# A mixture-of-experts stage on one core: 32-row blocks for the ranks with fewest tokens, 64 + 32 rows for middle ranks, and another order of experts

## The chip, the cores and the metric

The kernel runs on one core of one Trainium2 chip. The metric is device time in microseconds (us). Before the change the median of three runs is 1831.31 us (1824.54 to 1831.61). The profile is of one further execution, which took 1831.17 us; its first to last instruction span 1829.4 us.

## The reference

One decoder layer over 512 tokens of width 1024: two token mixers and a projection, a layer norm, then 32 experts of which each token takes 4, and a layer norm. The change concerns the experts alone.

```python
def moe_ffn(x2d, router_w, router_b, w1, b1, w2, b2):
    logits = (x2d @ router_w + router_b).astype(jnp.float32)      # 512 x 32
    top_logit, top_idx = lax.top_k(logits, TOP_K)                 # TOP_K = 4
    gate = jax.nn.softmax(top_logit, axis=-1)
    ...
    def expert_block(acc, blk):
        tok, w, e = blk
        h = x_pad[tok] @ w1[e] + b1[e]                            # 1024 -> 2048
        g, lin = jnp.split(h, 2, axis=-1)
        g = jnp.minimum(g, SWIGLU_LIMIT)
        lin = jnp.clip(lin, -SWIGLU_LIMIT, SWIGLU_LIMIT)
        act = g * jax.nn.sigmoid(SWIGLU_ALPHA * g) * (lin + 1.0)
        y = act @ w2[e] + b2[e]                                   # 1024 -> 1024
        return acc.at[tok].add((w[:, None] * y).astype(acc.dtype)), None
```

With the inputs of `setup_inputs()` the experts, expert 0 last and the others by falling count, have 179, 176, 152, 115, 106, 94, 89, 89, 85, 73, 73, 67, 61, 60, 57, 56, 54, 53, 48, 41, 40, 35, 34, 30, 28, 25, 20, 19, 18, 16, 15 and 40 tokens.

## The kernel before

A front part (until about 604 us) computes the mixers, the layer norm and the router. `Router.order` ranks experts 1 to 31 by their number of tokens; rank 31 (`FIRST`) is expert 0, which is always worked on first because its number is known ahead. `moe` then goes through the 32 ranks in the order that the string `TURNS` writes out (h heavy, m middle, l light). All weights are float32.

Each expert's weights come in 12 **units** of 1 MB, 8 of w1 and 4 of w2, fetched by SyncE's queue (SP) in the order in which they are used, into a ring of eight buffers (`Units.fetch`, L251; the tiles are called `raw` and, for two of the eight, `hl`). A **turn** is one pass of the main loop (L460): the first w1 half of this expert (4 units), two w2 units of the expert before, the second w1 half (4 units), the other two w2 units of the expert before. So a turn holds 8 units of its own expert and 4 of the expert of the turn ahead of it.

The tokens of an expert stand in **blocks** (`blocks`). A *full* block has 128 rows. Its operands are split into a high and a low float32r part: ScalarE makes the high part (L271), VectorE the low one (L274), and TensorE does three products of them (`PASS`), 12 matmuls of 128x512 for a unit (L392). A *half* block has 64 rows: 64 columns of TensorE hold the rows, the two halves of the outputs go to columns 0 to 63 and 64 to 127 at the same time, plain float32, no split (L380). A buffer is free again when a half block's matmuls, or a full block's split, have read it.

Before the change rank 0 has two full blocks, ranks 1 to 3 a full and a half block, ranks 4 to 12 and `FIRST` one full block, ranks 13 to 30 one half block. In the order of the turns: F l m l h l m l l h l m l m l h l m l l m l h l m l m l l m l l.

For each block `gather` builds a one-hot of the tokens (L320, VectorE), turns it into row numbers by four small matmuls (L325), and fetches the rows by an indirect DMA of GpSimd (L338) into the one tile `xg`; `turn` transposes them on TensorE (L360 half, L369 full). `swiglu` runs on VectorE and ScalarE (L425 to L430). `send` copies the product (L449) and adds it to the rows of `ysum` in DRAM by an indirect DMA (L450), all 128 partitions, 512 KB for a full block and 256 KB for a half one. `bias2` (after the first turn) adds the gated b2 rows. `early` (after the second) counts the tokens and writes a table (`overflow_table`) of experts with more tokens than their blocks hold; `overflow`, a loop behind the main one, runs once for each entry of the table.

Of the kernel before, what the change touches and what calls it, by code (L numbers as in the profile page):

```python
# [27 lines left out]
def moe_consts(nc, cp):  # L28
    c = {}
    ident = cp.tile([P, P], F32, name="ident")  # L30
    nc.gpsimd.memset(ident, 0.0)
    nc.gpsimd.affine_select(out=ident, in_=ident, compare_op=OP.not_equal, fill=1.0, base=0,
                            pattern=[[-1, P]], channel_multiplier=1)
    io1 = cp.tile([P, T], F32, name="io1")
    nc.gpsimd.iota(io1, pattern=[[1, T]], base=1, channel_multiplier=0,
                   allow_small_or_imprecise_dtypes=True)


    slots = cp.tile([P, 5], F32, name="slots")
    nc.gpsimd.iota(slots[:, 0:2], pattern=[[P, 2]], base=T, channel_multiplier=1,  # L40
                   allow_small_or_imprecise_dtypes=True)
    nc.gpsimd.iota(slots[:, 2:5], pattern=[[P, 3]], base=T, channel_multiplier=1,
                   allow_small_or_imprecise_dtypes=True)
    half = cp.tile([P, 2], F32, name="half")
    for k, v in enumerate((0.5 - P // 2, -P // 2)):
        nc.vector.tensor_scalar(half[:, k:k + 1], slots[:, 0:1], float(T + P // 2), float(v), op0=OP.is_ge, op1=OP.mult)
    for k in (2, 3):
        nc.vector.tensor_add(slots[:, k:k + 1], slots[:, k:k + 1], half[:, 0:1])
    nc.vector.scalar_tensor_tensor(slots[:, 4:5], slots[:, 4:5], float(1 - 2 * P), half[:, 1:2], op0=OP.add, op1=OP.add)
# [48 lines left out]
class Router:  # L98
# [3 lines left out]
    def __init__(self, nc, cp, wp, c, rw, gate, perm):  # L102
# [10 lines left out]
        self.permf = cp.tile([1, E], F32, name="permf")  # L113
# [57 lines left out]
    def order(self, wp, pp):  # L171
# [25 lines left out]
        nc.vector.tensor_copy(self.permf, pr[0:1])  # L197
# [82 lines left out]

DOUBLE, HEAVY, LIGHT = 1, 4, 18
# [4 lines left out]
def blocks(r):  # L286

    if r < HEAVY:
        return [P, P] if r < DOUBLE else [P, H2]
    return [H2] if FIRST - LIGHT <= r < FIRST else [P]  # L290


TURNS = "lmlhlmllhlmlmlhlmllmlhlmlmllmll"


def turns():

    kinds = dict(h=list(range(HEAVY)), m=list(range(HEAVY, FIRST - LIGHT)), l=list(range(FIRST - LIGHT, FIRST)))
    return [FIRST] + [kinds[k].pop(0) for k in TURNS]

# [5 lines left out]
def moe(tc, units, ahead, wr, wq, pp, ph, c, R, x1d, ysum, acc, w1, w2, B1, xg, early, bias2, last, xs, ne=E):  # L306
# [4 lines left out]
    x2 = x1d.rearrange("t (h d) -> (t h) d", h=2)  # L311
    y2 = ysum.rearrange("t (h d) -> (t h) d", h=2)

    def gather(r, b, fetch=True):


        m = blocks(r)[b]
        oh = wr.tile([P, NT, P], F32R, name="oh", bufs=1)
        for k in range(0, P, m):
            nc.vector.scalar_tensor_tensor(oh[:, :, k:k + m], R.pos1[:, :, r:r + 1].to_broadcast([P, NT, m]),  # L320
                                           -float(b * P), c["io1"][:, None, 0:m].to_broadcast([P, NT, m]), op0=OP.add,
# [15 lines left out]
        g, src, n = (xg, x1d, T) if m == P else (xg[:, 0:512], x2, 2 * T)  # L337
        nc.gpsimd.indirect_dma_start(out=g, out_offset=None, in_=src,  # L338
                                     in_offset=bass.IndirectOffsetOnAxis(ap=ix[:, 0:1], axis=0),
                                     bounds_check=n - 1, oob_is_err=False)  # L340
        return to, g

    def rows(oh):
# [6 lines left out]
        s = wr.tile([P, KD, H2], F32, name="xsl", bufs=2)  # L350
# [3 lines left out]
    def turn(src, pool, name):  # L354
        if src.shape[1] == 512:

            s = pool.tile([P, KD, H2], F32, name=name + "l", bufs=2 if name == "xs" else 1)
            tp = pp.tile([P, 4, P], F32, name="tp", bufs=2)
            for k in range(4):
                nc.tensor.transpose(tp[:, k, :], src[:, k * P:(k + 1) * P], c["ident"])  # L360
            nc.scalar.copy(s.rearrange("p (h k) t -> p k h t", h=2), tp.rearrange("p k (h t) -> p k h t", h=2))  # L361
            return s
        s = pool.tile([P, 2, KD, P], F32R, name=name, bufs=2)
# [31 lines left out]
    def room(x, hold, i, half):  # L395

        if x.dtype == F32:
            if half == 0:
                hold[i] = ph.tile([P, 2, 512], F32, name="h", bufs=2)
            return hold[i][:, half, :]  # L400
        return ph.tile([P, 2, 512], F32, name="h", bufs=2)

    def gemm1(r, ev, half, xs, hold):
        pick = c["sel0"] if r == FIRST else R.selh[:, r:r + 1]
        hs = []
        for i, x in enumerate(xs):
            h = room(x, hold, i, half)
            for n in range(2):
                c0 = (2 * half + n) * 512
                light = x.dtype == F32  # L410
                nc.tensor.matmul(h[n * H2:(n + 1) * H2] if light else h[:, n, :],
                                 pick.to_broadcast([P, H2 if light else P]), B1[:, c0:c0 + 512], start=True, stop=False)
# [30 lines left out]
    def send(ys, tos):  # L443

        for y, (_, ix) in zip(ys, tos):
            light = len(y.shape) == 2
            o = wq.tile([P, D], F32, name="yo", bufs=2)
            o, to, n = (o[:, 0:512], y2, 2 * (T + 2 * P)) if light else (o, ysum, T + 2 * P)
            nc.scalar.copy(o, y if light else y.rearrange("p a b -> p (a b)"))  # L449
            nc.gpsimd.indirect_dma_start(out=to, out_offset=bass.IndirectOffsetOnAxis(ap=ix[:, 0:1], axis=0),  # L450
                                         in_=o, in_offset=None, bounds_check=n - 1, oob_is_err=True,
# [3 lines left out]
    assert sorted(seq) == list(range(E)) and blocks(seq[1]) == blocks(seq[-1]) == [H2]  # L455

    assert all(len(blocks(b)) == 1 and blocks(b)[0] == H2 for a, b in zip(seq, seq[1:]) if len(blocks(a)) == 2)
    nc.vector.tensor_copy(R.perm, R.permf)
    pend = None
    for i, r in enumerate(seq):  # L460
# [10 lines left out]
        acts = [wq.tile([P, F], F32, name="act", bufs=2)[:, 0:F if n == P else 512] for n in blocks(r)]  # L471
# [34 lines left out]
    nc.vector.tensor_scalar(G, c["io1"], gt[:, 1:2], None, op0=OP.is_equal)  # L506
# [510 lines left out]
MORE = 16  # L1017
# [3 lines left out]
def overflow_table(nc, room, room2, R, tabd, tabs):  # L1021


    n96 = STEPS * E

    def take(*shape):
        nonlocal at
        n = 1
        for d in shape:
            n *= d  # L1030
        a = room[0:1, at:at + n]
        at += n
# [3 lines left out]
    b = take(STEPS, E)  # L1036
    ee = take(STEPS, E)
    kk = take(MORE + 1)
    for lo, hi, cap in ((0, DOUBLE, 2 * P), (DOUBLE, HEAVY, P + H2), (HEAVY, E, P),
                        (FIRST - LIGHT, FIRST, H2)):  # L1040
        if lo == hi:
            continue
        nc.gpsimd.iota(b[:, :, lo:hi], pattern=[[P, STEPS], [0, hi - lo]], base=cap, channel_multiplier=0,
                       allow_small_or_imprecise_dtypes=True)
# [24 lines left out]
    nc.vector.tensor_copy(res[:, 0, MORE:MORE + 1], cs[:, n96 - 1:n96])  # L1069
# [313 lines left out]
```

## Time and profile before

| what | value |
|---|---|
| median of three runs | 1831.31 us |
| the profiled execution | 1831.17 us, span 1829.4 us |
| TensorE (PE) busy | 1705.7 us, 93% |
| VectorE (DVE) busy | 1129.6 us, 62% |
| ScalarE (ACT) busy | 682.9 us, 37% |
| GpSimd (POOL) busy | 228.8 us, 13% |
| moved by DMA | 490.18 MB, mean 268 GB/s |
| mean granted TensorE clock | 0.967 |

Busy time counts a stretch once however many instructions overlap in it. The granted clock is a share of 2.4 GHz. The DMA share is the busy share of the core's 16 DMA engines; over short stretches it reads slightly over 1 when they are full.

### The profile page before, as it was taken

The numbers are of one execution on the slowest core, as the hardware profiler recorded it, in microseconds if no ns is written. First come the engines' busy times: TensorE is split into PE (matmuls) and PEld (weight loads), VectorE is DVE, ScalarE is ACT, GpSimd is POOL, SyncE is SP. The second block draws the span as 40 slices with busy tenths as digits, with TensorE's granted clock in tenths as the row PEclk, the third lists the DMA queues.
The fourth block names the chain that finished last, engine by engine and source line by source line (L and its number), as shares of the span: only waits on it lengthen the run. The fifth ranks groups of instructions, "written<-read, shape, count | busy, mean of one in ns | idle before, by whom it ended". The sixth has DMA issues, their size and how long they took to land. (4 is left out here: it accounts for less than half of the span.)

```text
span 1829.4 us, 20419 instructions
## 1 busy us (share of the span) xinstructions
PE 1705.7 (93%) x7476; PEld 1094.8 (60%) x7504; DVE 1129.6 (62%) x1564; ACT 682.9 (37%) x849; POOL 228.8 (13%) x157
## 2 busy tenths in 40 slices
PE   7999999899988989899999999999988999998982
PEld 5778878688877736566535555456544546544431
DVE  5999998967467648755444556546435546544424
ACT  4432452434343425334323434435223424433311
POOL 0210130123103001301010011101010101001001
PEclk9999999899999979999999999999999999999996
DMA  5213212122364559949899999979999889999992
GB/s 189 92 70 104 92 70 91 40 100 76 109 225 186 224 210 369 393 195 387 333 404 361 377 383 407 333 266 380 400 394 406 295 325 368 385 403 386 416 382 92
DMA packets 76826, 490.18 MB, mean 268 GB/s; under 512 B 9871, under 2 KB 10255, under 8 KB 21842
## 3 DMA queue, kind: packets, MB, share of 16 engines
q1 hardware_dynamic: 65042, 458.80, 63.5%
q0 software_dynamic: 8656, 21.10, 5.2%
q10 hardware_dynamic: 3024, 8.94, 1.3%
q8 instruction: 60, 0.98, 0.2%
q14 instruction: 44, 0.36, 0.1%
HBM read 472.62 MB, written 20.77 MB: 270 GB/s over the span
## 5 line engine op out<-in xcount | busy, mean ns | idle before, releaser
L274 DVE TENSOR_TENSOR hl<-raw,hl 128x1024 fp32r<-128x1024 f32 x345 | 421.0, 1254 | 113.2 <-ACT hl L271 112.3
L271 ACT CAST hl<-raw 128x1024 fp32r<-128x1024 f32 x345 | 348.6, 1048 | 203.4 <-PE mm L723 77.2
L392 PE MATMUL h<-hl,xs 128*128 128x512 f32 x1440 | 359.6, 403 | 9.0 <-ACT hl L271 4.9
L392 PEld LDWEIGHTS h<-hl,xs 128*128 128x128 f32 x1440 | 267.8, 190 | 101.4 <-issue 16.2
L723 PE MATMUL mm<-xhl,hl 128*128 128x512 f32 x1176 | 290.2, 401 | 8.7 <-ACT hl L271 8.7
L723 PEld LDWEIGHTS mm<-xhl,hl 128*128 128x128 f32 x1176 | 223.4, 191 | 64.1 <-ACT hl L271 9.4
L380 PE MATMUL h<-raw,xsl 128*64 128x512 f32 x1008 | 238.1, 598 | 2.0 <-DMA raw<-w 1.5
L392 PE MATMUL y<-hl,hs 128*128 128x512 f32 x672 | 185.2, 421 | 15.8 <-ACT hl L271 8.5
L780 DVE SCALAR_TENSOR_TENSOR acc<-zp,vec,acc 128x512 f32<-128x512 f32 x240 | 183.5, 779 | 2.0
L392 PEld LDWEIGHTS y<-hl,hs 128*128 128x128 f32 x672 | 127.3, 198 | 72.5 <-DVE hl L274 17.5
L380 PEld LDWEIGHTS h<-raw,xsl 128*64 128x64 f32 x1008 | 69.2, 136 | 125.3 <-issue 120.1
L429 DVE TENSOR_SCALAR gm<-h 128x512 f32<-128x512 f32 (+1 forms) x36 | 32.9, 914 | 179.5 <-PE h L380 96.8
L450 POOL DMA_INDIRECT ysum<-yo,idx x35 | 58.4, 1669 | 582.1 <-ACT yo L449 309.1
L338 POOL DMA_INDIRECT xg<-x1d,idx x34 | 57.5, 1692 | 479.6 <-DVE oh L320 346.4
L274 DVE TENSOR_TENSOR hl<-hl 128x1024 fp32r<-128x1024 f32 x80 | 94.7, 1219 | 23.5 <-ACT hl L271 22.9
L425 DVE TENSOR_SCALAR gm<-h 128x512 f32<-128x512 f32 (+1 forms) x36 | 32.8, 911 | 122.3 <-PE h L392 62.4
L380 PE MATMUL y<-raw,hsl 128*64 128x512 f32 x416 | 96.6, 599 | 1.3 <-ACT hsl L361 1.2
L271 ACT CAST hl<-hl 128x1024 fp32r<-128x1024 f32 x80 | 80.8, 1050 | 42.8 <-DMA hl<-w 25.9
L620 PE MATMUL mm<-hl,xhl 128*128 128x512 f32 x384 | 94.5, 398 | 1.7 <-ACT sg L773 1.5
L449 ACT COPY yo<-y 128x512 f32<-128x512 f32 (+1 forms) x31 | 24.2, 780 | 183.8 <-PE y L380 153.6
L620 PEld LDWEIGHTS mm<-hl,xhl 128*128 128x128 f32 x384 | 71.5, 188 | 18.6 <-ACT sg L773 1.8
L380 PE MATMUL h<-hl,xsl 128*64 128x512 f32 x336 | 81.1, 611 | 0.0
(315 smaller groups left out, 1592.1 us busy)
## 6 DMA issues: line engine op xcount, KB each, us to landing
raw<-w SPq DMA_DIRECT2D x288, 1024.0 KB, 8.8
hl<-w SPq DMA_DIRECT2D x96, 1024.0 KB, 9.2
raw<-wf SPq DMA_DIRECT2D x44, 1024.0 KB, 4.8
cvp<-xT SPq DMA_DIRECT2D x8, 256.0 KB, 5.8
hT<-x SPq DMA_DIRECT2D x1, 2048.0 KB
x1d<-hT ACTq DMA_DIRECT2D x4, 512.0 KB, 5.9
ysum<-hT ACTq DMA_DIRECT2D x4, 512.0 KB
hT<-ysum SPq DMA_DIRECT2D x1, 2048.0 KB
```

Of the source, the lines that this page charges most:

```text
L271: nc.scalar.copy(s[:, 0, :], w)
L274: eng.tensor_sub(s[:, 1, :], w, f32(s[:, 0, :]))
L338: nc.gpsimd.indirect_dma_start(out=g, out_offset=None, in_=src, in_offset=bass.IndirectOffsetOnAxis(ap=ix[:, 0:1], axis=0), bounds_check=n ...
L380: nc.tensor.matmul(o[j * H2:(j + 1) * H2], x[:, 2 * u + k, :], w[:, k * 1024 + j * 512:k * 1024 + (j + 1) * 512], start=first and k == 0, ...
L392: nc.tensor.matmul(o[:, j, :], x[:, a, 2 * u + k, :], s[k][:, b, j * 512:(j + 1) * 512], start=first and k == 0 and i == 0, stop=end and k ...
L425: nc.vector.tensor_scalar(gm, h, LIMIT, None, op0=OP.min)
L429: nc.vector.tensor_scalar(gm, h, LIMIT, -LIMIT, op0=OP.min, op1=OP.max)
L449: nc.scalar.copy(o, y if light else y.rearrange("p a b -> p (a b)"))
L450: nc.gpsimd.indirect_dma_start(out=to, out_offset=bass.IndirectOffsetOnAxis(ap=ix[:, 0:1], axis=0), in_=o, in_offset=None, bounds_check=n ...
L620: nc.tensor.matmul(ps, src[:, a, kk, t * P:(t + 1) * P], w[k][:, b, :], start=(kk == 0 and (a, b) == PASS[0]), stop=(kk == KD - 1 and (a, ...
L723: nc.tensor.matmul(ps, w[k][:, a, j * P:(j + 1) * P], mov[:, b, k, :], start=(k == 0 and (a, b) == PASS[0]), stop=(k == KD - 1 and (a, b) ...
L780: nc.vector.scalar_tensor_tensor(o, z[:, j:j + T], V("dw_w", m * CT + j), o, op0=OP.mult, op1=OP.add)
```

## The change

The blocks of each rank now stand in a table, `RANKS`. Rank 0 keeps two full blocks, ranks 1 to 3 a full and a half one, and ranks 4 to 7 and `FIRST` a full one. Ranks 8 to 12 get a half and a *quarter* block of 32 rows (kind n) instead of a full one, ranks 13 to 24 keep a half block, ranks 25 to 30 get one quarter block (kind s) instead of a half one. A quarter block uses 32 of TensorE's columns for each quarter of the outputs: four times two matmuls of 128x256 a unit, at columns 0, 32, 64 and 96. It gathers and sends 128 rows of 1 KB. The order of turns is F l h s l m n l h s l m l n h s l n s l n m l h s l n m l n l s l, with the heavy ranks in the order 1, 2, 0, 3. A second float32r block of an expert keeps its transposed activations in the tile of `xs`, so that `hs` has one buffer instead of two. The table of overflowing experts is worked out on 128 partitions at once, written to DRAM and read back.

```diff
-DOUBLE, HEAVY, LIGHT = 1, 4, 18
+RANKS = [(P, P)] + [(P, 64)] * 3 + [(P,)] * 4 + [(64, 32)] * 5 + [(64,)] * 12 + [(32,)] * 6 + [(P,)]
 FIRST = E - 1
...
-TURNS = "lmlhlmllhlmlmlhlmllmlhlmlmllmll"
+TURNS = "lhslmnlhslmlnhslslnmlhslnmlnlsl"
...
+    kinds = dict(h=[1, 2, 0, 3], m=list(range(4, 8)), n=list(range(8, 13)), l=list(range(13, 25)), s=list(range(25, 31)))
...
+    def width(m):
+        return F * m // P
...
-        if m == P:
-            nc.vector.tensor_scalar(ix, ps[:, 0:1], c["slots"][:, b:b + 1], None, op0=OP.add)
-        else:
-            nc.vector.tensor_scalar(ix, ps[:, 0:1], c["slots"][:, 2 + b:3 + b], 2.0, op0=OP.add, op1=OP.mult)
-            nc.vector.tensor_scalar(gt[:, 1:2], ps[:, 0:1], c["slots"][:, 4:5], None, op0=OP.add)
+        nc.vector.tensor_scalar(ix, ps[:, 0:1], c["slot"][at, m], float(n), op0=OP.add, op1=OP.mult)
...
-        s = pool.tile([P, 2, KD, P], F32R, name=name, bufs=2)
+        s = pool.tile([P, 2, KD, P], F32R, name=name, bufs=2 if name == "xs" else 1)
...
             if x.dtype == F32:
+                m = x.shape[2]
+                d = width(m)
                 for k in range(2):
-                    for j in range(2):
-                        nc.tensor.matmul(o[j * H2:(j + 1) * H2], x[:, 2 * u + k, :],
-                                         w[:, k * 1024 + j * 512:k * 1024 + (j + 1) * 512],
+                    for j in range(P // m):
+                        nc.tensor.matmul(o[j * m:(j + 1) * m], x[:, 2 * u + k, :],
+                                         w[:, k * 1024 + j * d:k * 1024 + (j + 1) * d],
                                          start=first and k == 0, stop=end and k == 1)
...
-            o = wq.tile([P, D], F32, name="yo", bufs=2)
-            o, to, n = (o[:, 0:512], y2, 2 * (T + 2 * P)) if light else (o, ysum, T + 2 * P)
+            o = wq.tile([P, D], F32, name="yo", bufs=2)[:, 0:d]
...
-    nc.vector.tensor_scalar(G, c["io1"], gt[:, 1:2], None, op0=OP.is_equal)
+    nc.vector.tensor_scalar(G[0:H2], c["io1"][0:H2], gt[0:H2, 1:2], None, op0=OP.is_equal)
+    nc.vector.tensor_scalar(gt[H2:P, 1:2], gt[H2:P, 1:2], -0.5, None, op0=OP.add)
+    nc.vector.tensor_scalar(G[H2:P], c["io1"][H2:P], gt[H2:P, 1:2], None, op0=OP.is_equal)
...
-    for k in range(0, MORE, g):
-        nc.vector.tensor_tensor(eq, cs[:, None, :].to_broadcast([1, g, n96]),
-                                kk[:, k:k + g].unsqueeze(2).to_broadcast([1, g, n96]), op=OP.is_equal)
-        nc.vector.tensor_tensor(eq, eq, cf[:, None, :].to_broadcast([1, g, n96]), op=OP.mult)
-        for i, v in enumerate((ee, pe, b)):
-            vf = v.rearrange("p a b -> p (a b)")
-            nc.vector.tensor_tensor(q2, eq, vf[:, None, :].to_broadcast([1, g, n96]), op=OP.mult)
-            nc.vector.tensor_reduce(res[:, i, k:k + g], q2, axis=AX.X, op=OP.add)
...
+    nc.vector.scalar_tensor_tensor(eq, cs, kk, cf, op0=OP.is_equal, op1=OP.mult)
+    for i, v in enumerate((ee, R.permf[:, None, :].to_broadcast([P, STEPS, E]), b)):
+        nc.vector.tensor_tensor(q.rearrange("p (a b) -> p a b", a=STEPS), eq.rearrange("p (a b) -> p a b", a=STEPS), v,
+                                op=OP.mult)
+        nc.vector.tensor_reduce(res[:, 4 if i == 2 else i:5 if i == 2 else i + 1], q, axis=AX.X, op=OP.add)
...
+    nc.sync.dma_start(tabd.rearrange("o k -> k o"), res[0:MORE, 4:5])
+    nc.sync.dma_start(tabi.rearrange("o v k -> k (o v)"), ints[0:MORE])
+    nc.sync.dma_start(tabs, tabi)
```

Three places show what the new order does to the instructions. The first is TensorE in the turn behind the first heavy expert. Before, that turn is a light one behind rank 0; `h` and `y` are the accumulators of w1 and w2, `xsl` and `hsl` the transposed operands of a half block, `xs` and `hs` those of a full one, and the 16 matmuls of 64x512 are its first four units:

```order
L325 MATMUL tp<-vals,oh 128x4 x4
L411 LDWEIGHTS selh
L411 MATMUL h<-B_3596,selh 64x512
...
L380 MATMUL h<-raw,xsl 64x512 x16
L369 MATMUL tp<-ident,act 128x128 x8
...
L392 MATMUL y<-hl,hs 128x512 x2
L369 MATMUL tp<-ident,act 128x128 x4
```

In the changed kernel it is a turn with a quarter block behind rank 1 (`xs_5095` is its operand):

```order
L330 MATMUL tp<-vals,oh 128x4 x4
L420 LDWEIGHTS selh
L420 MATMUL h<-B_3618,selh 32x256
...
L388 MATMUL h<-raw,xs_5095 32x256 x32
L375 MATMUL tp<-ident,act 128x128 x8
L400 MATMUL y<-hl,hs 128x512 x4
```

Sixteen matmuls of 64 columns and 512 outputs became 32 of 32 columns and 256 outputs, for the same four units; the transposes of the heavy expert's activations and its w2 matmuls follow them as before.

The second place is TensorE in the first turn with 64 + 32 rows, where a full block stood before. `xs_5746` is the half block's operand and `xs_5770` the quarter block's:

```order
L375 MATMUL tp<-ident,act 128x128 x4
L388 MATMUL h<-raw,xs_5746 64x512 x4
L388 MATMUL h<-raw,xs_5770 32x256 x8
L375 MATMUL tp<-ident,act 128x128 x4
L388 MATMUL h<-raw,xs_5746 64x512 x4
L388 MATMUL h<-raw,xs_5770 32x256 x8
L388 MATMUL h<-hl,xs_5746 64x512 x4
L388 MATMUL h<-hl,xs_5770 32x256 x8
```

A unit is now four matmuls on 64 columns and then eight on 32, in turn, where a full block had twelve on 128.

The third place is SyncE's queue in the third turn. Here `raw` and `hl` are the buffers of the units, and the names that begin with `tab` belong to the table of `early`. Before, one write of the table stands behind the 55th fetch of a unit:

```order
L251 DMA raw<-w 128x2048
L251 ISA
L251 DMA hl<-w 128x2048
L1072 DMA tabd<-act 1x16
L251 ISA
L251 DMA hl<-w 128x2048
```

In the changed kernel two writes stand behind the 30th fetch, and the read back two fetches later:

```order
L253 DMA raw<-w 128x2048
L1082 DMA tabd<-act 24x1
L1083 DMA tabi<-act 24x4x1
L253 ISA
L253 DMA hl<-w 128x2048
L253 ISA
L253 DMA hl<-w 128x2048
L1084 DMA tabs<-tabi 1x96
```

The queue works in order, so the fetches below these rows wait for what these rows wait for.

## Rows read from the trace of the kernel before

**Rows 1.** The page, span cut in 40 slices: TensorE's granted clock and DMA.

```profile
span 1829.4 us, 20419 instructions
...
PEclk9999999899999979999999999999999999999996
DMA  5213212122364559949899999979999889999992
```

**Rows 2.** Windows: length, busy us (and instructions) by engine, clock, DMA share, GB/s.

```profile
core 0: us, PE busy (x) PEld busy (x) DVE busy (x) ACT busy (x) POOL busy (x), PEclk, DMA share, GB/s
640.00:690.00 50.00, 43.55 (x125) 17.87 (x127) 22.85 (x37) 11.10 (x17) 2.60 (x7) 0.73 0.56 211
690.00:765.00 75.00, 72.45 (x327) 46.32 (x329) 69.04 (x124) 35.63 (x39) 19.32 (x6) 0.98 0.99 397
765.00:890.00 125.00, 122.44 (x554) 84.69 (x557) 66.79 (x74) 47.72 (x53) 9.96 (x7) 0.99 0.77 288
890.00:965.00 75.00, 70.45 (x326) 31.40 (x324) 31.55 (x46) 23.27 (x29) 9.48 (x7) 1.00 1.02 407
965.00:1065.00 100.00, 99.69 (x443) 55.41 (x445) 53.62 (x58) 41.12 (x47) 9.82 (x5) 1.00 0.94 359
1065.00:1140.00 75.00, 69.76 (x311) 40.50 (x312) 42.58 (x50) 29.55 (x35) 7.25 (x5) 1.00 1.02 410
1140.00:1265.00 125.00, 120.31 (x532) 64.17 (x534) 65.08 (x80) 49.70 (x59) 10.66 (x7) 0.97 0.87 322
1415.00:1515.00 100.00, 99.21 (x437) 49.04 (x437) 51.14 (x57) 37.25 (x43) 7.19 (x4) 1.00 0.86 319
1515.00:1765.00 250.00, 231.90 (x1030) 128.89 (x1035) 119.91 (x139) 90.07 (x106) 23.19 (x16) 0.99 1.00 392
```

**Rows 3.** What SyncE's queue waited for, 690 to 1765 us: total, times, longest.

```profile
SPq L251 <- PE h L380: 363.6, 161, 11.7
SPq L251 <- DVE hl L274: 249.3, 97, 12.9
SPq L251 <- PE y L380: 231.0, 65, 15.8
```

**Rows 4.** DMA issues (KB, us to landing) and the indirect queue's packets, MB, share.

```profile
raw<-w SPq DMA_DIRECT2D x288, 1024.0 KB, 8.8
...
q0 software_dynamic: 8656, 21.10, 5.2%
```

**Rows 5.** Timeline of TensorE in a heavy turn: start, us, matmuls.

```profile
957.65 1.94 PE L380 MATMUL h<-raw,xsl 128*64 128x512 f32 x8
959.52 3.06 PE L392 MATMUL h<-hl,xs 128*128 128x512 f32 x12
962.51 1.94 PE L380 MATMUL h<-raw,xsl 128*64 128x512 f32 x8
```

**Rows 6.** Timeline of TensorE's weight loads in a light turn.

```profile
1641.90 0.14 PEld L380 LDWEIGHTS h<-hl,xsl 128*64 128x64 f32 x2 [0.29 <-issue]
1642.33 0.14 PEld L380 LDWEIGHTS h<-raw,xsl 128*64 128x64 f32 x2 [0.28 <-issue]
```

**Rows 7.** Groups by form: count, busy us, mean ns of one.

```profile
L325 PE MATMUL tp<-vals,oh 128*128 128x4 f32 x144 | 21.6, 249 | 1.6 <-DVE xs L371 1.6
L369 PE MATMUL tp<-ident,act 128*128 128x128 f32 x120 | 18.0, 286 | 0.5 <-DVE act L430 0.5
L411 PE MATMUL h<-B,selh 128*64 128x512 bf16 x84 | 16.9, 397 | 9.2 <-DVE gm L425 8.4 <-DVE gm L429 0.8
```

**Rows 8.** Timeline of TensorE, ten small matmuls of the router between two large ones.

```profile
615.22 0.19 PE L215 MATMUL tp<-selrb,tri 128*128 128x32 bf16 x1
...
615.46 0.18 PE L215 MATMUL tp<-selrb,tri 128*128 128x32 bf16 x1
```

**Rows 9.** Groups of VectorE, 690 to 770 us: count, busy us, mean ns.

```profile
L1067 DVE TENSOR_TENSOR yo<-yo,act 1x256 f32<-1x256 f32 x24 | 9.8, 409 | 0.5
L1068 DVE TENSOR_REDUCE act<-yo 1x2 f32<-1x256 f32 x24 | 9.7, 404 | 0.5
```

More of the change, by code (lines that the diff above doesn't have):

```diff
@@ L36, in moe_consts @@
                    allow_small_or_imprecise_dtypes=True)
[L39 to L49, printed above, removed]
+    keys = sorted({b for r in range(E) for b in blocks(r)})
+    slots = cp.tile([P, len(keys)], F32, name="slots")
+    step = cp.tile([P, 2], F32, name="step")
+    c["slot"] = {}
+    for i, (first, m) in enumerate(keys):
+        s = slots[:, i:i + 1]
+        nc.gpsimd.iota(s, pattern=[[0, 1]], base=T + first, channel_multiplier=1, allow_small_or_imprecise_dtypes=True)
+        nc.vector.tensor_copy(step[:, 1:2], s)
+        for k in range(1, P // m):
+            nc.vector.tensor_scalar(step[:, 0:1], step[:, 1:2], float(T + first + k * m), m / P - m, op0=OP.is_ge,
+                                    op1=OP.mult)
+            nc.vector.tensor_add(s, s, step[:, 0:1])
+        c["slot"][first, m] = s
     ones = cp.tile([P, P], BF, name="ones_bf")
     nc.vector.memset(ones, 1.0)
-    c.update(ones=ones, ident=ident, io1=io1, slots=slots)
+    c.update(ones=ones, ident=ident, io1=io1)
     return c
@@ L286, in blocks @@
 def blocks(r):
-    if r < HEAVY:
-        return [P, P] if r < DOUBLE else [P, H2]
-    return [H2] if FIRST - LIGHT <= r < FIRST else [P]
-TURNS = "lmlhlmllhlmlmlhlmllmlhlmlmllmll"
+    rows = RANKS[r]
+    return [(sum(rows[:b]), rows[b]) for b in range(len(rows))]
+TURNS = "lhslmnlhslmlnhslslnmlhslnmlnlsl"
 def turns():
-    kinds = dict(h=list(range(HEAVY)), m=list(range(HEAVY, FIRST - LIGHT)), l=list(range(FIRST - LIGHT, FIRST)))
+    kinds = dict(h=[1, 2, 0, 3], m=list(range(4, 8)), n=list(range(8, 13)), l=list(range(13, 25)), s=list(range(25, 31)))
     return [FIRST] + [kinds[k].pop(0) for k in TURNS]
@@ L399, in room @@
                 hold[i] = ph.tile([P, 2, 512], F32, name="h", bufs=2)
-            return hold[i][:, half, :]
+            return hold[i][:, half, 0:width(x.shape[2])]
         return ph.tile([P, 2, 512], F32, name="h", bufs=2)
@@ L407, in gemm1 @@
             h = room(x, hold, i, half)
[L408 to L412, printed above, removed]
+            m = x.shape[-1]
+            d = min(width(m), 512)
+            for n in range(F // d):
+                c0 = half * F + n * d
+                nc.tensor.matmul(h[:, n, :] if m == P else h[n * m:(n + 1) * m], pick.to_broadcast([P, m]),
+                                 B1[:, c0:c0 + d], start=True, stop=False)
             hs.append(h)
@@ L476, in moe @@
             pe, pa, pg = pend
-            hs = [turn(a, wq, "hs") for a in pa]
+            hs = [turn(a, *((wr, "xs") if b and a.shape[1] == F else (wq, "hs"))) for b, a in enumerate(pa)]
             ys = places(hs)
@@ L1035, in overflow_table @@
     at = 0
[L1036 to L1043, printed above, removed]
+    b, ee, cand = take(STEPS, E), take(STEPS, E), take(STEPS, E)
+    cs, eq, q, res, kk = take(n), take(n), take(n), take(5), take(1)
@@ L1044, in overflow_table @@
+    caps = [sum(x) for x in RANKS]
+    lo = 0
+    while lo < E:
+        hi = lo
+        while hi < E and caps[hi] == caps[lo]:
+            hi += 1
+        nc.gpsimd.iota(b[:, :, lo:hi], pattern=[[P, STEPS], [0, hi - lo]], base=caps[lo], channel_multiplier=0,
                        allow_small_or_imprecise_dtypes=True)
+        lo = hi
     nc.gpsimd.iota(ee, pattern=[[0, STEPS], [1, E]], base=0, channel_multiplier=0, allow_small_or_imprecise_dtypes=True)
-    nc.gpsimd.iota(kk, pattern=[[1, MORE + 1]], base=1, channel_multiplier=0, allow_small_or_imprecise_dtypes=True)
@@ L1338, in body @@
     mo.close()
[L1340 removed]
+    again = nc.values_load(tabs[0:1, 3, 0:1], min_val=0, max_val=1)
     with tc.For_i(0, again, 1):
```

117 lines of the change are left out of this document (60 added, 57 removed).

## The prediction

> **What bounds the kernel now.** I read the slices of the page first: from the 16th slice on (686 us) the DMA engines are at 9 tenths in most slices, with dips in a few, and the granted clock is at 9 or more [rows 1]. So both transfers and TensorE are near their limits in the expert stage, and the windows have to say which one gives the pace where. In the calm windows (890 to 965, 1065 to 1140) the DMA share is 1.02 at 407 and 410 GB/s while TensorE is idle for 6 and 7 per cent: transfers set the pace there. In the others (765 to 890, 965 to 1065, 1140 to 1265, 1415 to 1515) TensorE is busy for 96 to 99.7% and the share falls to 0.77, 0.94, 0.87 and 0.86: TensorE sets the pace, and the DMA engines stand idle [rows 2]. Each of these four windows holds the turn of one heavy expert. SyncE's queue shows why: it waits 595 us for matmuls of half blocks and 249 us for splits to give a buffer back [rows 3], so at a heavy expert all eight buffers are full and no transfer can run ahead.
>
> Counted as 1.02 less the share, times the length, the DMA engines lose 2 us in 690 to 765, then 31, 8, 19 and 16 us in the four heavy windows, and 5 us in 1515 to 1765 [rows 2]: about 81 us after 690. That, and the transfers themselves, is all that the change can win there.
>
> **A walk over the turns.** The cost of a turn for the transfers: an expert is 12 units of 1.0486 MB, 12.58 MB, and its share of the indirect queue's 21.10 MB over 34 gathers, 0.62 MB [rows 4]; at 408.5 GB/s that is 32.3 us.
>
> The cost for TensorE: in a heavy turn the period of a unit is 962.51 - 957.65 = 4.86 us; the full block's twelve matmuls take 962.51 - 959.52 = 2.99, which I put at 2.9 without the change of shape, and the half block's part 1.87 [rows 5]. In a light turn two loads of weights start every 0.43 us, and a unit has four such pairs, 1.72 us [rows 6]. Per block there are, besides, transposes (0.15 us each, 16 for a full block, 8 for a half), four gathering matmuls (0.15) and four bias matmuls (0.2 to 0.4) [rows 7]: estimates of 4.5 us for a full block and 2.7 for a half. A turn is 8 units of its own, 4 of the expert before, and its blocks' 4.5 or 2.7.
>
> How far can TensorE fall behind before transfers stop? Eight buffers are 8 x 32.3 / 12 = 21.5 us of transfers, of which 8.8 us go until a unit has landed [rows 4]: 12.7 us. So I carry a lag from turn to turn: add the turn's TensorE time less 32.3; below 0 TensorE waits; what goes beyond 12.7 is idle time of the DMA engines. Behind rank 0: a heavy turn of 62.3 us, then a light one of 39.7 (it holds w2 of the heavy expert), then a middle one of 34.6: idle 33.5. Behind ranks 1 to 3: 53.0, 35.9 and 34.6: idle 13.9, 20.4 and 13.9. The sum is 81.7, where the windows show 33 (with 690 to 765), 8, 19 and 16, and 5 elsewhere. The walk is thus good to some 6 us in a place and to a few in all.
>
> **The price of a quarter block is the unknown.** No row shows four column groups at once. From below: two groups halve the time of one, since their matmuls start together; four would halve it again, 0.86 us a unit. For it speaks that the two loads of a pair lie within 0.14 us [rows 6], so column groups load side by side, and that ten small matmuls of the router start in 615.22 to 615.46, 27 ns apart [rows 8]: a group of four needs one matmul each 53 ns. From above: if only two of the four ran at once, a unit would cost as much as a half block's, 1.72 us. I take 0.86, since the nearest row (two groups) shows no loss: 0.43 us a pair for 512 outputs in both passes. Its own small work is 1.7 us (half the transposes and the bias, the same gathering).
>
> **The sum.** The same walk for the changed order, started with full buffers, since 640 to 690 is a stretch of small work in which the DMA share is 0.56 [rows 2]:
> - first heavy expert, now rank 1: 53.0 us, then 8 x 0.86 + 4 x 4.86 + 1.7 = 28.0, then a light turn behind a quarter block, 13.8 + 3.4 + 2.7 = 19.9. The lag peaks in the heavy turn: idle 16.5 (33.5 before);
> - second and fourth, with a lag of 3.3 ahead of them: 3.3 + 20.7 - 12.7 = 11.3 each (13.9 each before);
> - third, now rank 0: 62.3 and 4 us for w2 of a 64 + 32 expert, 66.4; 1.1 + 34.1 - 12.7 = 22.5 (20.4 before);
> - a turn with 64 + 32 rows: 8 x (1.72 + 0.86 + 0.18 for two changes of shape) + 6.9 + 4.4 = 33.4 behind a light one, where a middle one takes 34.6: never above the limit. Two changes of shape a unit are priced by the heavy unit: 4.86 - 2.9 - 1.72 = 0.24, rounded down as the fill is shorter.
>
> That is 61.6 instead of 81.7: **-20 us**.
>
> Transfers: the eleven experts with quarter blocks send 128 KB less each, 1.44 MB in all. The indirect queue's 21.10 MB hold the 16 engines for 5.2% of 1829.4 us, 4.5 us a MB [rows 4]: -6.5 us if time goes with bytes, 0 if it goes with packets (64 + 32 needs one more send each): **-5**.
>
> The table: 48 of its VectorE instructions take 19.5 us [rows 9], in a window where VectorE is busy 69 of 75 us and TensorE loses 2.5 [rows 2]. Nearly all of it goes: **-2** (0 to -5).
>
> Its DMAs: the two writes stand behind the 30th fetch and wait for VectorE work that follows the heavy expert's first w1 half, and SyncE then holds the next fetches. Buffers that came free in that half (a unit each 4.86 us) stay empty so long: 0 to 10 us, **+3**. The read back waits for a landing, which two later fetches cover.
>
> The start has some 17 more small VectorE instructions between its splits; VectorE waits there for ScalarE anyway. The end has two more, on the path: together **+1**. The single `hs` buffer costs nothing: two experts whose first block is a full one never follow each other.
>
> -20 - 5 - 2 + 3 + 1 = -23 us: 1831.2 - 23 = **1808 us**. The profiled execution (1831.17) stands at the median (1831.31).
>
> **A rule against it.** The trace's two column groups run without loss against each other [rows 6]. The Trainium skill, *TensorE: Matmul & The Clock Gate*, Part 3, gives a measured speedup of 2.38 for three column groups, 79% of three. By that a quarter block's unit would cost 1.08 us, the walk would lose 70.5 us, and the sum would be -14: 1817 us. No row here shows more than two groups.
>
> **Rivals.**
> 1. *Quarter blocks cost nearly as much as half ones.* At 1.33 us a unit the walk gives 86 us of idle transfers, 4 more than before: the sign turns there, after the other terms near 1833. At 1.72 us light experts win nothing, each 64 + 32 expert costs TensorE 12 x 3.62 against 12 x 2.9, and the walk gives 125 us: 81.7 becomes 125, +43 - 5 + 2 = **1871 us**, slower. For it: no row shows four groups. Against: the close loads and starts of [rows 6, 8].
> 2. *Transfers are the bound whatever TensorE does.* The calm windows already run at 1.02; if the four heavy windows kept their idle time (because the lag builds in the heavy turn itself, which does not change), only -5 - 2 + 4 would remain: **1828 us**. Against: what follows the heavy turn adds 13 us at the first and 6 at the others in the walk.
> 3. *More than I count:* if the lag that buffers can carry is 18 us and not 12.7, the walk gives 47 us for the changed order and 78.5 for the old one, -32; with 5 for the table, -32 - 5 - 5 + 4 = -38: **1793 us**. The 8 us of 965 to 1065, below the walk's 13.9, speak for it.
> 4. *The clock.* TensorE is busy for 15.5 us in a 32.3 us turn where a quarter block follows a light one (twice). The granted clock was 0.73 in 640 to 690, with TensorE busy 87% [rows 2]. At 1.2 GHz such a turn takes 31 us, still inside the transfers: 0 to +5 where a heavy turn follows closely. It is in the range only.
> 5. *The blocks overflow*: excluded by the counts. The table fits every rank (85 in 96, 60 in 64, 25 in 32), so the loop behind the main one does not run.
>
> **Chances and range.** Quarter blocks near 0.86, 1790 to 1822 us: 0.68, with rival 3 in it. Between 1.0 and 1.25, 1812 to 1826: 0.11. Rival 2 and the like, 1822 to 1838: 0.10. Rival 1, 1835 to 1875: 0.11. A measurement of this kernel tells about 0.5%, 9 us, from no change. Below 1822: 0.68 and most of 0.11, less a little, 0.73. Within 9 us: 0.15. Above 1840: 0.12. The range leaves out a tenth on either side: 1782 to 1838; the likeliest case alone is 1790 to 1822.
>
> **What would show it.** Right: eight matmuls of 32x256 in near 0.86 us with starts a few ns apart in fours; DMA shares near 1.0 in the turns behind the heavy ones, and some 60 us of idle transfers after 690; no gap in the fetches at the table's writes beyond 10 us. Wrong: a unit of a quarter block above 1.3 us, or TensorE busy throughout the 64 + 32 turns with the share below 0.9.

## The result and the profile after

The changed kernel took **1802.8 us** (median of 4 runs, 1798.7 to 1806.6) beside 1831.5 us for the kernel before: ratio 0.9851, 95% interval 0.9818 to 0.9884. The profiled execution took 1804.05 us with a span of 1802.2, 27 us less than the one of before. The page of the changed kernel, the same slices as [rows 1] and the row of the indirect queue ([rows 4]):

```profile
span 1802.2 us, 22812 instructions
...
PEclk9999999899999869999999999999899999999986
DMA  5222221122255656999989999589999899999992
...
q0 software_dynamic: 9104, 19.66, 4.8%
```

DMA engines are again at 9 tenths in most slices, and there are still dips: one slice at 5, some at 8. The windows of the changed kernel, cut where [rows 2] is cut (us, busy us and instructions of PE, PEld, DVE, ACT and POOL, granted clock, DMA share, GB/s):

```profile
690.00:765.00 75.00, 74.08 (x443) 42.19 (x442) 41.45 (x62) 28.27 (x33) 7.19 (x5) 1.00 0.87 306
765.00:890.00 125.00, 117.47 (x678) 59.27 (x678) 50.69 (x75) 36.54 (x47) 14.28 (x11) 0.97 1.01 402
890.00:965.00 75.00, 74.57 (x444) 37.75 (x442) 35.74 (x41) 26.66 (x33) 9.20 (x5) 1.00 0.88 336
965.00:1065.00 100.00, 90.53 (x478) 48.32 (x474) 44.00 (x57) 32.27 (x39) 17.32 (x8) 0.97 1.02 409
1065.00:1140.00 75.00, 71.45 (x410) 37.14 (x409) 28.73 (x42) 21.07 (x26) 6.61 (x5) 0.95 0.94 374
1140.00:1265.00 125.00, 111.78 (x798) 65.83 (x798) 38.05 (x58) 25.19 (x36) 12.24 (x9) 0.97 0.83 325
1265.00:1415.00 150.00, 137.29 (x794) 64.34 (x792) 58.90 (x81) 43.90 (x57) 19.28 (x12) 0.97 1.02 406
1415.00:1515.00 100.00, 92.64 (x568) 46.61 (x566) 36.17 (x49) 25.29 (x32) 12.19 (x6) 0.99 0.89 339
1515.00:1740.00 225.00, 206.24 (x1298) 87.31 (x1296) 59.45 (x94) 42.04 (x60) 24.96 (x16) 0.94 1.00 391
```

Counted as in the prediction (1.02 less the share, times the length), the first heavy expert loses 11.3 + 1.3 us of transfers, the second 10.5, rank 0 (1065 to 1265) 6 + 23.8, the fourth 13, the rest 4.5: 70 us, where [rows 2] gave 81. Packet by packet the same comes out. From 690 us to the landing of the last weight I take 1.02 times the length less all packets' time over 16 engines: 81.6 us idle before, 70.7 after. The packets' own time fell too, from 1031.0 to 1016.3 us: the indirect queue's by 8.6, the weights' by 6.9.

The price that was disputed stands in the timeline of TensorE, where a heavy expert's last matmuls meet a quarter block and its successor (start, us, tile, shape, count):

```profile
969.87 1.07 PE L388 MATMUL h<-hl,xs 128*32 128x256 f32 x16
970.76 1.05 PE L388 MATMUL h<-raw,xs 128*32 128x256 f32 x16
...
1180.86 3.63 PE L388 MATMUL h<-raw,xs 128*32 128x256 f32 x64
```

64 matmuls from start to end in 3.63 us are four units. From the start of the first matmul to that of the next unit's first they take 0.863 us, in groups of four whose starts lie 3 to 7 ns apart, a group each 216 ns.

### The profile page after: what moved, and what is told of

Its sections match the earlier page's. It is cut to its first block, busy times and chain, and to the rows that moved or that the text cites. A ratio compares the mean times of both kernels' runs of the same rounds, so it can differ in the third digit from the quotient of the medians.

```text
span 1802.2 us, 22812 instructions
## 1 busy us (share of the span) xinstructions
PE 1660.1 (92%) x8840; PEld 1008.7 (56%) x8840; DVE 956.0 (53%) x1431; ACT 557.5 (31%) x739; POOL 237.4 (13%) x174
## 5 line engine op out<-in xcount | busy, mean ns | idle before, releaser
L276 DVE TENSOR_TENSOR hl<-raw,hl 128x1024 fp32r<-128x1024 f32 x261 | 324.3, 1269 | 133.9 <-ACT hl L273 132.5
L273 ACT CAST hl<-raw 128x1024 fp32r<-128x1024 f32 x261 | 265.0, 1047 | 218.5 <-PE mm L742 78.2
L388 PE MATMUL h<-raw,xs 128*32 128x256 f32 (+1 forms) x2016 | 299.0, 499 | 20.9 <-DMA raw<-w 20.8
L400 PE MATMUL h<-hl,xs 128*128 128x512 f32 x1008 | 255.4, 407 | 14.5 <-ACT hl L273 10.2
L400 PEld LDWEIGHTS h<-hl,xs 128*128 128x128 f32 x1008 | 190.6, 193 | 80.1 <-ACT hl L273 16.3
L388 PEld LDWEIGHTS h<-raw,xs 128*32 128x32 f32 (+1 forms) x2016 | 94.5, 125 | 189.9 <-issue 134.9
L438 DVE TENSOR_SCALAR gm<-h 128x512 f32<-128x512 f32 (+2 forms) x41 | 30.7, 749 | 225.6 <-PE h L388 162.0
L388 PE MATMUL y<-raw,hs 128*32 128x256 f32 (+1 forms) x848 | 128.5, 500 | 9.3 <-DMA raw<-w 8.7
L434 DVE TENSOR_SCALAR gm<-h 128x512 f32<-128x512 f32 (+2 forms) x41 | 30.7, 748 | 192.0 <-PE h L388 157.1
L400 PE MATMUL y<-hl,hs 128*128 128x512 f32 x432 | 118.2, 419 | 6.7 <-DVE hl L276 3.6
L388 PE MATMUL h<-hl,xs 128*32 128x256 f32 (+1 forms) x672 | 102.3, 498 | 3.8 <-DMA hl<-w 3.8
```

The source lines that it names most:

```text
L273: nc.scalar.copy(s[:, 0, :], w)
L276: eng.tensor_sub(s[:, 1, :], w, f32(s[:, 0, :]))
L388: nc.tensor.matmul(o[j * m:(j + 1) * m], x[:, 2 * u + k, :], w[:, k * 1024 + j * d:k * 1024 + (j + 1) * d], start=first and k == 0, stop=e ...
L400: nc.tensor.matmul(o[:, j, :], x[:, a, 2 * u + k, :], s[k][:, b, j * 512:(j + 1) * 512], start=first and k == 0 and i == 0, stop=end and k ...
L434: nc.vector.tensor_scalar(gm, h, LIMIT, None, op0=OP.min)
L438: nc.vector.tensor_scalar(gm, h, LIMIT, -LIMIT, op0=OP.min, op1=OP.max)
```

## The experiments

Ratios are against the kernel before on the same chip, and "idle" is the idle time of transfers, counted from packets as above. A difference of 0.001 between two ratios is 1.8 us.

| run | us | ratio, 95% interval | idle, us |
|---|---|---|---|
| the change | 1802.8 | 0.9851 [0.9818, 0.9884] | 70.7 |
| s_only | 1811.8 | 0.9910 [0.9889, 0.9931] | 69.9 |
| n_only | 1830.6 | 0.9999 [0.9983, 1.0015] | 95.7 |
| order_only | 1852.9 | 1.0122 [1.0098, 1.0146] | 99.2 |
| rest_only | 1825.4 | 0.9967 [0.9948, 0.9985] | 72.5 |
| old_places | 1784.7 | 0.9765 [0.9748, 0.9782] | 56.7 |
| walk_order | 1786.3 | 0.9778 [0.9759, 0.9797] | 51.5 |
| n64 | 1823.8 | 0.9969 [0.9951, 0.9987] | 85.1 |
| late_table | 1802.4 | 0.9869 [0.9847, 0.9892] | 72.0 |
| late_tied | 1800.6 | 0.9840 [0.9820, 0.9860] | 71.8 |
| rank0_light | 1796.6 | 0.9823 [0.9797, 0.9850] | 65.7 |
| no_send32 | 1800.1 | 0.9828 [0.9803, 0.9853] | 77.5 |
| old_late | 1781.3 | 0.9730 [0.9708, 0.9753] | 55.0 |

**The change taken apart: s_only, n_only, order_only, rest_only.** Each starts from the changed kernel and puts back part of it:

```
 # s_only:     ranks 8 to 12 full blocks again
-... [(64, 32)] * 5 + [(64,)] * 12 + [(32,)] * 6 ...
+... [(P,)] * 5 + [(64,)] * 12 + [(32,)] * 6 ...
 # n_only:     ranks 25 to 30 half blocks again
+... [(64, 32)] * 5 + [(64,)] * 12 + [(64,)] * 6 ...
 # order_only: both;  rest_only: both, and the TURNS and kinds of before
+... [(P,)] * 5 + [(64,)] * 12 + [(64,)] * 6 ...
```

> Edit: ranks 8 to 12 are full blocks again (no 64 + 32), all else as changed. Theory (quarter blocks behind the heavy experts take TensorE's lag away; a 64 + 32 expert costs TensorE as much as a full block, 2.87 against 2.85 us a unit): the same idle time of the DMA engines, and, since a 64 + 32 expert issues two gathers and two sends of 128 packets each, transfers equal or 3 us shorter: 1797 to 1804 us, 1800. Rival A (fewer bytes in the indirect queue give the gain, 128 KB for each quarter block, some 14 us over eleven): 5 of 11 are lost, 1809. Rival B (the order of experts gives it): 1803.

> Edit: ranks 25 to 30 are half blocks again, 64 + 32 and the order stay. Theory: behind a heavy expert TensorE has 8 x 0.86 us more to do, the walk's idle time rises from 63 to 86 us, and the sends of six blocks are twice as wide, 4 to 7 us: 1825 to 1837, 1831 us, so no faster than the kernel before. Rival A (bytes): 6 of 11 are lost, 1811. Rival B (order): 1803.

> Edit: both block tables as before the change (full, half), with the new order, the new table code and the rest. Theory: the walk gives 85 us of idle time against 77 for the order of before, since each heavy expert is now 20 to 25 turns of the same two kinds with less slack behind it: 1825 to 1837, 1829. Rival A (bytes): 1818. Rival B (order): 1803 to 1806.

> Edit: blocks and order as before the change; what is left is the table with a candidate in each row of the tile, its two writes and the read-back, the slots, the single hs buffer. Theory: VectorE's 48 table operations go (-2), SyncE's hold adds up to 7: 1825 to 1836, 1830. Rival C (the shorter table is worth more than the blocks, since its 27 us of VectorE stood ahead of splits): 1815 or less. Rival B: 1831.

Measured: rest -6 us; the order on top of it **+28** (1.0122 - 0.9967); both kinds of new blocks on top of that **-50**. The new order by itself makes the kernel slower, which rules out that the order gives the gain. Fewer bytes do not give it either: s_only alone would fit that rival (1811.8 beside its 1809, and outside the theory's 1797 to 1804), but n_only, with 6 of 11 quarter blocks fewer, should then have come to 1811 and took 1831. With 64 + 32 in place, quarter blocks win 27 us, of which idle transfers are 25 (95.7 to 70.7), where the theory had 23; with full blocks in place they win 39. That step is shown. What I had not expected is the 64 + 32 block: it wins 11 us (0.9910 to 0.9851) and, without quarter blocks, 23, though its unit costs TensorE the same as a full block's. And the order cost 28 us where my walk gave 8, so that order_only lies outside all its ranges. Some of that has a place: the heaviest expert, rank 0, stood first among the heavy ones and behind a light one; now it stands third and behind a 64 + 32 expert, in order_only a full block. The window of order_only that holds it (columns as above):

```profile
1140.00:1265.00 125.00, 121.75 (x551) 82.64 (x551) 61.04 (x68) 45.51 (x52) 10.71 (x7) 0.99 0.76 275
```

and the one of rest_only that holds it at its old place:

```profile
765.00:890.00 125.00, 124.76 (x581) 84.48 (x581) 67.25 (x73) 48.80 (x55) 12.33 (x8) 1.00 0.82 316
```

That is 32.5 us of idle transfers against 25. Some 10 us more lie at ranks 1 and 2, which stand first in the new order: their windows in order_only, from 690 to 1065 us, lose 37 us, and in rest_only (965 to 1065, 1140 to 1265) 27. The window that opens this stretch has a share of 0.84 in order_only,

```profile
690.00:765.00 75.00, 74.72 (x354) 42.55 (x354) 41.03 (x61) 28.31 (x33) 7.02 (x5) 1.00 0.84 297
```

and of 1.01 in rest_only.

**Where the heavy experts stand: old_places, walk_order.**

```
-TURNS = "lhslmnlhslmlnhslslnmlhslnmlnlsl"    # h = 1, 2, 0, 3
+TURNS = "lmlhsmllhsmlmlhsnllnlhsnlnslnsl"    # old_places, h = 0, 1, 2, 3
+TURNS = "lnlshsmlmnlnllmlmlhsshsnllnlhsl"    # walk_order, h = 1, 0, 2, 3
```

> Edit: all blocks as changed; the heavy experts at the places and in the sequence of before (rank 0 first, at turns 4, 9, 15 and 22), each with a quarter-block expert right behind it. Theory (the order alone lost 27 us, because the places leave TensorE's lag too little room to fall between them; the blocks won it back): the walk gives 46 us of idle transfers against 63 for the changed kernel, so 1776 to 1792 us, 1785. Rival (the order loses nothing with the new blocks, the 27 us belong to full blocks alone): 1798 to 1808.

> Edit: only the sequence of experts, taken from a search with the walk: rank 0 third among the heavy ones, with a half block before and two quarter blocks behind; no 64 + 32 expert right before a heavy one but one. Theory (the walk): 34 us of idle transfers against 63: 1768 to 1785 us, 1775. Rival (idle time that the walk doesn't see, some 7 us more in the changed kernel, belongs to the 64 + 32 experts' late matmuls and goes as well): 1765 to 1770. Rival (transfers now set the pace nearly everywhere): 1785 to 1800.

With the heavy experts at their old places the new blocks give 1784.7 us, on the walk's number: the order costs 16 us (0.9851 - 0.9765) with the new blocks too. The windows of old_places at the four heavy experts:

```profile
765.00:890.00 125.00, 123.53 (x716) 87.45 (x714) 69.94 (x78) 49.49 (x59) 11.50 (x8) 1.00 0.85 330
...
965.00:1065.00 100.00, 95.23 (x584) 55.76 (x581) 57.46 (x70) 39.33 (x50) 12.59 (x8) 1.00 0.97 375
...
1140.00:1265.00 125.00, 122.63 (x742) 64.38 (x742) 54.84 (x74) 40.50 (x50) 13.23 (x9) 0.99 0.88 329
...
1415.00:1515.00 100.00, 97.94 (x694) 48.13 (x694) 37.04 (x58) 24.59 (x35) 10.86 (x8) 1.00 0.92 357
```

They lose 21, 5, 18 and 10 us, against 31, 8, 19 and 16 in [rows 2], with the heavy turns at the same places and quarter blocks behind them. walk_order lies 11 us above its forecast: the walk gave 34 us of idle transfers and 51.5 came. So the walk ranked two orders rightly that it had 17 us apart (63 and 46), and not the next two, 12 us apart (46 and 34), which took the same time.

**Why 64 + 32 wins: n64.** Two half blocks cost TensorE 3.44 us a unit, but, like 64 + 32, need no split of the weights into two parts by ScalarE and VectorE.

```
-... [(64, 32)] * 5 ...
+... [(64, 64)] * 5 ...
-        s = pool.tile(..., name=f"{name}{P // n}", bufs=2 if name == "xs" else 1)
+        s = pool.tile(..., name=f"{name}{P // n}", bufs=2)
```

> Edit: ranks 8 to 12 in two half blocks (64 + 64) instead of 64 + 32, a second buffer for their transposed activations. It asks why 64 + 32 won 9 us over full blocks, and 22 where the light experts are half blocks, though a unit costs TensorE the same 2.87 and 2.85 us. Theory S (a full block's weights are split by ScalarE and VectorE, and TensorE waits for the splits, 33 us in the order-only run against 18 with 64 + 32): no splits here either, so the gain stays apart from 0.57 us a unit more TensorE work, partly hidden: 1803 to 1820. Rival W (TensorE's work alone): a unit of 3.44 us, the walk's idle time 93 against 63: 1828 to 1838, well above the 1812 of full blocks. Rival I (the narrower sends of the 32-row blocks give it): 1806 to 1812 by 128 KB more for each expert, with nothing else moved.

It fell outside all three ranges, between those of S and W: 11 us above full blocks, where TensorE's work alone gives 30. TensorE's waits (engine, tile and line, and what it waited for: total us, times, longest), first in order_only, 690 to 1760 us:

```profile
PE h L400 <- ACT hl L273: 13.2, 10, 2.2
...
PE h L400 <- DVE hl L276: 9.4, 13, 1.6
PE y L400 <- DVE hl L276: 7.5, 12, 0.9
...
PE y L400 <- ACT hl L273: 2.7, 3, 1.2
```

and the same in n64:

```profile
PE h L400 <- ACT hl L273: 7.4, 3, 3.1
...
PE y L400 <- DVE hl L276: 2.9, 5, 0.8
...
PE h L400 <- DVE hl L276: 1.2, 2, 0.8
```

A full block's matmuls wait for `hl`, the split weights. These rows sum to 33 us in order_only, 31 in s_only, 18 in n_only, 20 in the changed kernel, 13 in n64 (with 1.2 of a fourth row). So five experts without splits save TensorE 11 to 18 us of waiting, which is the size of what 64 + 32 wins and of what n64 lost less than its work.

The size is all that speaks for the waits as the cause; their place speaks against it. In order_only the window with most of them, 10.7 us, is one in which transfers set the pace (share 1.00):

```profile
1540.00:1760.00 220.00, 203.74 (x906) 117.86 (x904) 119.44 (x133) 90.15 (x105) 24.70 (x13) 0.98 1.00 386
PE h L400 <- ACT hl L273: 3.6, 3, 2.2
PE h L400 <- DVE hl L276: 3.6, 5, 1.6
PE y L400 <- DVE hl L276: 2.3, 4, 0.9
PE y L400 <- ACT hl L273: 1.2, 1, 1.2
```

Rank 0's window, 1140 to 1265 us, with a share of 0.76, has 0.8 us of them. Counted wait by wait, 31.7 of 32.8 us in order_only, 30.6 of 31.1 in s_only and 19.9 of 20.4 in the changed kernel lie where the share of the 15 us around the wait is 0.95 or more. Nor is the win of 64 + 32 idle time: from s_only to the change idle time goes from 69.9 to 70.7 us, and from order_only to n_only it falls by 3.5. What falls is the packets' own time, by 6 us in the first pair and by 17 in the second, of which the weights' packets are 5 and 14. No run made the splits alone faster. Why 64 + 32 wins stays open.

**The table's DMAs: late_table, late_tied.** The first edit issued the three DMAs in later turns of the code, and the scheduler put them back to the same place: they stood at 707 us in SyncE's queue. The second tied them to values of those turns:

```
-    nc.sync.dma_start(tabd..., res[0:MORE, 4:5])     # behind the table, with tabi and tabs
+        if i == 6:
+            for o, j in ((k5, 5), (k4, 4)):
+                nc.vector.scalar_tensor_tensor(o, gtn[0][0][:, 0:1].to_broadcast([P, j]), 0.0, R.kept[:, 0:j],
+                                               op0=OP.mult, op1=OP.add)
+            ...                                       # the two writes, from k5 and k4
+        if i == 7:
+            ...                                       # tabs[0] from gtn, then the read-back
```

> Edit: the table's entries are copied to two small tiles of their own, and the three DMAs of the table go to SyncE's queue in turn 5 (the two writes) and turn 9 (the read-back) instead of right behind the table. Theory (SyncE's wait of 7.9 us for the write, in which the DMA share falls to 0.10 in 700 to 710 us, costs transfers that TensorE later waits for): 4 to 9 us less, 1794 to 1799. Rival (the first heavy expert's lag hides it, as there TensorE sets the pace): 1801 to 1805, no change.

> Edit: as in the run before it, but the table's writes depend on a value of turn 7 and its read-back on one of turn 8, so that they stand behind fetches of that time in SyncE's queue (the earlier edit left them at 707 us, where the changed kernel has them: it tested nothing). Theory (SyncE's hold at the table costs transfers): the DMA share of 0.10 in 700 to 710 us rises, 4 to 9 us less than the changed kernel, 1794 to 1799. Rival (what the hold takes is hidden, since TensorE sets the pace at the first heavy expert): 1800 to 1805.

No change in either. late_table left the DMAs where they were, so it tests nothing; in late_tied the writes stand at 841 us and the read-back at 868, and SyncE waits 2.8 us for them. SyncE's wait for the read-back in the changed kernel was

```profile
SPq L1084 <- DMA tabi<-act: 7.9, 1, 7.9
```

The windows of the changed kernel at the table (columns as above):

```profile
700.00:710.00 10.00, 9.72 (x52) 6.09 (x52) 8.29 (x21) 3.85 (x5) 1.06 (x1) 1.00 0.10 25
710.00:720.00 10.00, 10.00 (x47) 5.73 (x45) 6.55 (x8) 5.01 (x6) 0.00 (x0) 1.00 1.08 300
```

and of late_tied:

```profile
700.00:710.00 10.00, 9.72 (x50) 7.99 (x49) 8.14 (x9) 6.16 (x7) 1.07 (x1) 1.00 0.40 83
710.00:720.00 10.00, 10.00 (x50) 4.66 (x50) 7.55 (x21) 3.53 (x4) 1.06 (x1) 1.00 0.67 255
```

The hole of 0.10 fills to 0.40, and the next stretch gives back as much (1.08 to 0.67): TensorE is busy for 9.7 to 10 us of 10 in all four rows, sets the pace, and the transfers idle a little sooner or later. The hold is hidden. SyncE's 7.9 us of waiting looked expensive and cost nothing.

**Rank 0's place: rank0_light.**

```
-TURNS = "lhslmnlhslmlnhslslnmlhslnmlnlsl"
+TURNS = "lhslmnlhslmnlhslslnmlhslnmlnlsl"
```

> Edit: the half block and the 64 + 32 expert right before rank 0 change places, nothing else. Theory (rank 0's place lost 7 us more than the walk says, since the 64 + 32 expert's last w2 matmuls stand behind rank 0's first w1 half and hold buffers for 16 us): SyncE's longest waits there fall, 5 to 10 us less, 1793 to 1798. Rival (the walk alone: two more us of lag carried over): 1800 to 1803.

1796.6 us, 5 less, and 5 us less idle time, but the intervals of the two ratios overlap. The wait that I named was still there. SyncE's waits from 1090 to 1190 us in the changed kernel:

```profile
SPq L253 <- PE y L388: 41.7, 8, 16.2
SPq L253 <- PE h L388: 22.8, 9, 3.6
```

and in rank0_light:

```profile
SPq L253 <- PE y L388: 40.4, 7, 14.5
...
SPq L253 <- PE h L388: 16.6, 10, 3.9
```

Its longest wait for w2 matmuls (`y`) fell from 16.2 to 14.5 us only: whatever expert stands ahead of rank 0, its w2 matmuls follow the heavy half turn. So the time lies in the theory's range and its mechanism is not settled; a swap of two experts is worth at most a few us.

**What the indirect queue's time is worth: no_send32.**

```
             nc.scalar.copy(o, y)
+            if d == 256:
+                continue
```

> Edit: the eleven sends of quarter blocks are left out, so the rows of those blocks are missing from the sum. It asks what the indirect queue's time is worth: 11 x 128 packets of 1024 bytes at 104 ns are 9.2 us of the 16 engines. Theory (transfers set the pace in most turns, so their time counts in full outside the heavy places): 5 to 9 us less, 1794 to 1798. Rival (it counts only where DMA engines aren't idle anyway, and sends fit into gaps): 1800 to 1805.

The indirect packets took 9.4 us less (84.2 to 74.8), and idle time rose by 6.8 (70.7 to 77.5): the end came 3 to 4 us earlier, with overlapping intervals. In the profiled execution the last weight landed no sooner, at 1758.3 us and not at 1755.7; only the end behind it was shorter. Time taken out of the queue here mostly turned into idle time.

**The fastest: old_late**, old_places with the tied table of late_tied.

> Edit: the heavy experts at the places of before with a quarter block behind each (1785 us) and the table's DMAs tied to turns 7 and 8. Theory (hold costs transfers): there the table's hold lies two turns ahead of the first heavy expert, in turns where transfers set the pace, so 3 to 8 us less, 1777 to 1782, the fastest so far. Rival (hidden): 1783 to 1787.

1781.3 us, ratio 0.9730 [0.9708, 0.9753]: the fastest here, 1.2 points below the change. Against old_places the intervals just overlap, so whether the tied table adds anything is open.

## Why the prediction came out

The total was right: 1808 forecast, 1802.8 measured, -23 against -27 between the profiled executions. The mechanism of the quarter blocks was right as well: behind a heavy expert they let TensorE catch up, and 25 us of idle transfers go with them (n_only). Several sizes were not right, and that the total came out so near is in part luck. The order by itself cost 28 us where the walk of the expectations gave 8, and the new blocks then won 50 where it gave 22 and the transfers 5: two misses of 20 and 23 us that cancel.

- **The price of a quarter block**: 0.86 us a unit taken, 0.863 measured. Starts of a group lie 3 to 7 ns apart, so four column groups ran at once without loss. By an estimate from the Trainium skill's figure (*TensorE: Matmul & The Clock Gate*, Part 3: a speedup of 2.38 with three column groups, 79% of three) it would have been 1.08; the 0.863 of this trace does not agree with carrying that share over to four groups of 32 columns. Rival 1 is gone with the measured 0.863.
- **A unit with 64 + 32 rows**: 2.76 taken, 1.867 + 1.001 = 2.87 measured; the two changes of shape cost 0.28 us together and not 0.18.
- **"Never above the limit"**, a turn with 64 + 32 rows for nothing: this step failed. It prices such a turn by TensorE's work alone, the same as a full block's, and so gave the new blocks no gain of their own; they won 11 to 23 us in the runs. What the step leaves out is open: the waits for a full block's splits have the size but not the place.
- **Idle transfers, -20**: mis-sized; -11 by packets (81.6 to 70.7), and 9 of these 11 are in rest_only already (72.5), which has neither the blocks nor the order. The blocks took idle time away (99.2 to 70.7) and the order had put nearly as much in (72.5 to 99.2). Place by place: first heavy expert 12.6 (16.5 forecast), second 10.5 (11.3), fourth 13 (11.3), rank 0 29.8 (22.5), and 5 elsewhere.
- **Transfers, -5**: mis-sized; -15 by packets. The indirect queue gave 8.6: packets of 1024 bytes took 104 ns on the mean, of 2048 bytes 178, of 4096 bytes 241 after the change and 265 before (gathers and sends together). Weights gave 6.9: packets above 500 ns hold 34.3 us of the 16 engines' time where they held 43.7. Neither is a cause of its own: no_send32 shows such time turning into idle time. So the two terms are best read together, -25 forecast and -26 by packets (over the share of 1.02: -25 of time), with rest_only's part in it.
- **The table and the rest, +2** (-2 + 3 + 1): -6 by rest_only, which has the table, its DMAs, the row numbers and the single `hs` buffer together. That most of it is the table's work of [rows 9] is argued. In rest_only the window of the first heavy expert, 765 to 890, has a DMA share of 0.82 where [rows 2] had 0.77, 6 us, and VectorE's table is short there too; the two go together, and no run parted them. late_tied shows the hold of SyncE hidden: the DMAs cost nothing that shows.
- **Behind the last weight**: 48.6 us before, 46.5 after, where +1 was forecast for start and end.
- **Rivals**: transfers as the bound whatever TensorE does (1828) would have needed idle time to stay with more or less work behind the heavy turns; with quarter blocks it fell by 25 to 29 us (n_only to the change, order_only to s_only). A lag of 18 us (47 us of idle time) did not show: 70.7. The clock: a granted 0.94 to 1.00 in the windows of after, and where it is lowest (1515 to 1740) the DMA share is 1.00, so it cost nothing there. But it also fell right ahead of rank 0's idle stretch, which is 1.7 us of TensorE's work at most (0.83 over 10 us, rows below), inside rival 4's 0 to 5. The loop for blocks that overflow did not run.

```profile
1120.00:1130.00 10.00, 9.86 (x40) 8.09 (x41) 7.05 (x8) 4.63 (x6) 0.00 (x0) 0.83 1.01 388
1130.00:1140.00 10.00, 10.00 (x47) 8.24 (x46) 6.74 (x9) 5.87 (x6) 1.05 (x1) 1.00 0.45 172
```

What the prediction never priced is the order by itself. Its walk was made for the changed order as a whole. Taken alone, the order lost 28 us with old blocks and 16 with new ones. The gain of the change is that of its blocks (-50 with the new order), less what the order took. Why the order took so much with full blocks, three times the walk's 8 us, stays open: its idle time has places (rank 0, and ranks 1 and 2 at the start), but no run parts the causes there.

## What to carry to other kernels

When a change has two parts that meet in one schedule, walk each part alone before the sum: here the new blocks were worth 50 us and their new order cost 16 to 28. And before a wait is priced, ask what sets the pace in that stretch: a queue held for 8 us beside a TensorE that is busy 10 of 10 us cost nothing, and a sum of TensorE's waits, such as the 33 us for split weights, is no price where most of them lie in stretches that transfers pace.

## What the runs showed of the hardware

Four groups of 32 columns at once took half the time of two groups of 64 for a unit (0.863 against 1.717 us), without a loss that the trace can show. Changing between the two shapes costs: a unit of 64 + 32 rows takes 1.867 + 1.001 us, 0.28 more than its two parts alone. Weight packets above 500 ns are not spread evenly: in order_only there are 95 in 1450 to 1500 us, where TensorE sets the pace (DMA shares of 0.71 to 0.83), and 3 in 1300 to 1350 us, where the share is 1.02. So the long packets stood beside idle transfers here. Whether one makes the other was not tested, and the reason wasn't looked for.
